# Plain strips in place of some 2x2 sum pairs, and another order of chunks, in a two-layer decoder kernel

## Chip, cores and metric

The kernel runs on one core of a Trainium2 chip. The metric is the device time of one execution in microseconds (us). The engines are TensorE (PE in the profile, with its weight loads as PEld), VectorE (DVE), ScalarE (ACT), GpSimd (POOL) and SyncE (SP), which issues the loads.

## What is computed

Two decoder layers over 256 tokens of width 2048, all in f32:

```python
for i in range(DEPTH):                      # DEPTH = 2
    h = rms_norm(x, pre_mix_gain[i])
    m = hybrid_mixer(h, ...)                # h @ w_in, attention and a gated recurrence, @ w_out
    x = x + rms_norm(m, post_mix_gain[i])
    h = rms_norm(x, pre_ffn_gain[i])
    f = (silu(h @ w_ffn_gate[i]) * (h @ w_ffn_up[i])) @ w_ffn_down[i]     # width 5632
    x = x + rms_norm(f, post_ffn_gain[i])
    gate = sigmoid(rms_norm(x, ple_gain[i]) @ w_ple_gate[i])
    x = x + (p[i] @ w_ple_proj[i]) * gate
```

## The kernel before

The 256 tokens are two tiles of 128 (`t` = 0, 1). The activations of a product stand transposed in SBUF (`xT`, four tiles `ck` of four 128-row blocks each, split into a high and a low part); they are the stationary operand, and weights stream past them. A weight **chunk** is 256 rows by 512 columns, 512 KB, loaded by SyncE into `wr` (6 buffers). ScalarE rounds it to the high part `wh` (L281), VectorE subtracts that to get the low part `wl` (L291); both have 7 buffers. One product of a chunk with one token tile is two blocks times three matmuls (high by high, low by high, high by low): 6 matmuls of 128x512.

`strip` (L306 to L309) makes 512 output columns: for each chunk, 6 matmuls for `t` = 0 and 6 for `t` = 1, in two PSUM banks `acc0` and `acc1`. With `skew=n` the second tile lags n chunks behind the first. At the end of each tile it calls `done(t, ps)`.

`paired` (L361) makes two such strips at once and saves one product in eight on the first two chunks of the two strips, by sums of blocks, in the manner of Strassen and Winograd. Its part `fast` (L398) takes four chunks, `r11`, `r12`, `r21`, `r22`, and forms four differences of them (`sub`, L396, VectorE, written over `wr`). It splits seven operands instead of four (L281 and L291), and takes sums of activation blocks that `mixed` (L332) made once per stage (L343, L349, L179, L180). It makes seven products of 6 matmuls into four banks `accc`, `acce`, `acca`, and two of the pool `ms` (rows `ms<-wh,sum` and `ms<-wh,ck`). Three results are copied out (L389), two are added (L426, L427). The part `plain` (L430) does the other chunks of each strip like `strip`. At the end `summed` (L357) adds what was copied out to the bank before `done` goes on. So one pair of nch chunks a strip has 4 nch - 1 products: 186 matmuls at nch = 8, 138 at nch = 6, 90 at nch = 4, where two strips would have 192, 144 and 96.

Each layer runs these stages in order: eleven strips of `w_in` with attention and recurrence between them; `w_out` as two pairs; the gated blocks `gated(n)`, n = 0 to 10, each a pair of a gate strip and an up strip; after blocks 2, 4, 7 and 10 the down product of that group of 2, 3, 3 and 3 blocks, as two pairs (columns s = 0, 1 and s = 2, 3; nch is 4 in the first group and 6 in the others); and the stage called PLE here, `w_ple_gate`, as two pairs, each with two short strips `projected` of 12 matmuls for p.

At two places of a layer the new activations come only from what has just ended: `post_norm` (L465) needs the squares of the whole row (L175 on ScalarE, sums and a power on GpSimd), then scales and adds on VectorE (L470), and `next_in` transposes the result on TensorE (L201, 32 blocks, tiles x_84 to x_87 for t = 0 and x_88 to x_91 for t = 1) and splits it (L208 on ScalarE, L210 on VectorE). This is so between `w_out` and the first gated block, and between the last down product and PLE. Such work is put off by `later(n, ...)`, n ticks of the chunk loop. In the first pair after such a border (`first=False`) `plain` of the first strip ran ahead of `fast`, from chunk 2 on and with skew 5, and the sums came 6 ticks later.

A gated block's result goes through DRAM to be transposed (`shuffled`), and is split at L179 and L180 into the `ck` tiles of the down product.

The program is written in this order, and a scheduler then places each engine's instructions; within that order it moves matmuls past one another where it expects a wait.

Of the kernel before, what the change touches and what calls it, by code (L numbers as in the profile page):

```python
# [17 lines left out]
NT = 2  # L18
# [29 lines left out]
def decoder(ctx: ExitStack, tc: tile.TileContext, x, p, positions, w_in, attn_sinks,  # L48
# [312 lines left out]
    def paired(lhs, sums, wa, wb, cols, done_a, done_b, nch=8, row0=0, first=True,  # L361
               skews=(0, 0), after=None):
# [35 lines left out]
        def fast(bank_e, bank_a):  # L398
# [11 lines left out]
            e = bank_e or psum("acce")  # L410
# [10 lines left out]
            a = bank_a or psum("acca")  # L421
# [8 lines left out]
        def plain(w, col, banks, skew, end):  # L430
            n = nch - 2
            ws = {}
            for i in range(n + skew):
                if i < n:
                    ws[i] = load_w(w, base + 2 + i, col)
                    acc(banks[0], block(2 + i, 0), ws[i])
                    if i == n - 1:
                        end(0)
                if i >= skew:
                    acc(banks[1], block(2 + i - skew, 1), ws[i - skew])  # L440
                tick()
            end(1)

        if first:
            e, a, c, x1, x2 = fast(None, None)
            if after:
                after()
            plain(wa, cols[0], (e, a), skews[0], lambda t: done_a(t, (e, a)[t], x1[t]))
        else:
            e, a = psum("acce"), psum("acca")  # L450
            plain(wa, cols[0], (e, a), skews[0], lambda t: None)
            e, a, c, x1, x2 = fast(e, a)
            for t in range(NT):
                done_a(t, (e, a)[t], x1[t])
            if after:
                after()
        d = psum("accd")
        plain(wb, cols[1], (c, d), skews[1], lambda t: done_b(t, (c, d)[t], x2[t]))
# [204 lines left out]
    for l in range(DEPTH):  # L663
# [427 lines left out]
        def gated(n, last, first):  # L1091
# [21 lines left out]
            paired(xT, lambda: sx[0], w_ffn_gate[l], w_ffn_up[l], (col, col), summed(done_gate),  # L1113
                   summed(done_up), first=n > 0, skews=(0 if n else SKEW, 0))

        for gi, glen in enumerate(FF_GROUPS):
# [11 lines left out]
            for s in range(4):  # L1128
# [37 lines left out]
        px = []  # L1166
        later(6, lambda: px.append(mixed(xT[0], ("kv", "A"))))

# [4 lines left out]
        def gate_of(s, pj):  # L1173
# [23 lines left out]
            return summed(done)  # L1197
# [38 lines left out]
```

## Time and profile before

| | |
|---|---|
| median of 2 runs | 2414.31 us (2413.87 to 2414.75) |
| the profiled execution | 2413.03 us, of which the span of instructions is 2411.3 us |
| PE busy | 2373.9 us, 98% of the span |
| PEld busy | 1955.5 us, 81% |
| DVE busy | 2044.5 us, 85% |
| ACT busy | 1382.8 us, 57% |
| DMA | 497.64 MB, mean 206 GB/s |

Busy is the share of the span in which an engine has an instruction under way. Matmuls overlap in the pipeline, so a busy PE need not be going at its full rate; the distance between the starts of two matmuls shows that.

### The profile page before, as it was taken

The page shows a single profiled execution, that of the slowest core. Times are in us where ns is not written, and L with a number is a line of the kernel's source. Part 1 is how long each engine was busy: PE and PEld are TensorE (multiplying, and loading weights), DVE is VectorE, ACT ScalarE, POOL GpSimd, SP SyncE. Part 2 cuts the span into 40 slices and gives each one's busy share as a digit, 9 for nine tenths or more (in the row PEclk, how much of TensorE's full clock was granted, in tenths as well). Part 3 has the DMA queues.
Part 4 walks back from the last instruction along what each step waited for, and adds up shares of the span by engine and source line. Part 5 has one row for each costly group of instructions (what it writes and reads, how often), then busy time and mean ns, then how long its engine had stood idle before and what let it go on. Part 6 is the DMA issues. An engine that isn't in the chain of part 4 may idle for free.

```text
span 2411.3 us, 31504 instructions
## 1 busy us (share of the span) xinstructions
PE 2373.9 (98%) x10975; PEld 1955.5 (81%) x10975; DVE 2044.5 (85%) x2689; ACT 1382.8 (57%) x1954; POOL 103.8 (4%) x213
## 2 busy tenths in 40 slices
PE   9999999999999999999999999999999999999999
PEld 7888887888888888877788888878888888888777
DVE  7687987899997898899877879788998988888996
ACT  6555466656555555557556554565555555555664
POOL 3100001000000000001010000010000000000010
PEclk9999999999999999999999999999999999999999
DMA  8666464776667666665776564746667576666744
GB/s 295 212 193 201 137 223 137 237 225 221 206 207 248 195 216 221 226 215 166 238 223 213 174 218 134 234 134 220 220 218 219 198 248 195 209 230 213 232 153 150
DMA packets 299360, 497.64 MB, mean 206 GB/s; under 512 B 23456, under 2 KB 69440, under 8 KB 299200
## 3 DMA queue, kind: packets, MB, share of 16 engines
q1 hardware_dynamic: 298896, 495.54, 63.5%
q8 instruction: 86, 1.41, 0.2%
q14 instruction: 74, 0.61, 0.1%
q10 hardware_dynamic: 240, 0.07, 0.0%
q0 software_dynamic: 64, 0.02, 0.0%
HBM read 470.38 MB, written 25.17 MB: 206 GB/s over the span
## 4 chain that ended last, share of the span: by engine, by line
PE 84%; DVE 9%; DMA 3%; ACT 2%; issue 2%; SPq 1%; POOL 0%; DVEq 0%; ACTq 0%; POOLq 0%
PE acc L306 7%; PE acc L307 7%; PE acc L309 6%; PE accc L383 5%; PE accc L384 5%; PE accc L380 5%; PE acca L383 5%; PE acca L384 5%; PE acca L380 5%; PE acce L384 4%; PE acce L380 4%; PE acce L383 4%; PE accd L383 4%; PE accd L384 4%; PE accd L380 4%; DVE wl L291 3%
## 5 line engine op out<-in xcount | busy, mean ns | idle before, releaser
L281 ACT CAST wh<-wr 128x1024 fp32r<-128x1024 f32 x978 | 1009.9, 1052 | 784.5 <-DVE wr L396 262.5
L291 DVE TENSOR_TENSOR wl<-wr,wh 128x1024 fp32r<-128x1024 f32 x978 | 1167.1, 1220 | 222.8 <-ACT wh L281 208.3
L306 PE MATMUL acc<-wh,ck 128*128 128x512 f32 x704 | 278.2, 395 | 0.8 <-ACT ck L179 0.8
L307 PE MATMUL acc<-wh,ck 128*128 128x512 f32 x704 | 275.5, 392 | 0.0
L309 PE MATMUL acc<-wl,ck 128*128 128x512 f32 x704 | 275.0, 391 | 0.0
L396 DVE TENSOR_TENSOR wr<-wr 128x1024 f32<-128x1024 f32 x184 | 225.0, 1223 | 6.8 <-DMA wr<-in_w_ffn_down_dram 1.7
L380 PE MATMUL acca<-wh,ck 128*128 128x512 f32 x564 | 222.6, 395 | 6.3 <-ACT wh L281 4.8
L383 PE MATMUL acca<-wh,ck 128*128 128x512 f32 x564 | 221.5, 393 | 3.5 <-DVE ck L180 1.8
L383 PE MATMUL acce<-wh,ck 128*128 128x512 f32 x564 | 220.6, 391 | 3.6 <-DVE ck L210 3.4
L380 PE MATMUL acce<-wh,ck 128*128 128x512 f32 x564 | 220.8, 392 | 0.4 <-ACT wh L281 0.4
L384 PE MATMUL acca<-wl,ck 128*128 128x512 f32 x564 | 221.0, 392 | 0.0
L384 PE MATMUL acce<-wl,ck 128*128 128x512 f32 x564 | 219.9, 390 | 0.3
L380 PE MATMUL accd<-wh,ck 128*128 128x512 f32 x472 | 184.0, 390 | 0.0
L380 PE MATMUL accc<-wh,ck 128*128 128x512 f32 x472 | 183.9, 390 | 0.0
L383 PE MATMUL accd<-wh,ck 128*128 128x512 f32 x472 | 183.8, 389 | 0.0
L383 PE MATMUL accc<-wh,ck 128*128 128x512 f32 x472 | 183.8, 389 | 0.0
L384 PE MATMUL accd<-wl,ck 128*128 128x512 f32 x472 | 183.7, 389 | 0.0
L384 PE MATMUL accc<-wl,ck 128*128 128x512 f32 x472 | 183.6, 389 | 0.0
L306 PEld LDWEIGHTS acc<-wh,ck 128*128 128x128 f32 x704 | 132.1, 188 | 27.6 <-ACT ck L179 1.0
L309 PEld LDWEIGHTS acc<-wl,ck 128*128 128x128 f32 x704 | 132.2, 188 | 27.4
L307 PEld LDWEIGHTS acc<-wh,ck 128*128 128x128 f32 x704 | 132.3, 188 | 27.0 <-DVE ck L180 0.4
L380 PEld LDWEIGHTS acca<-wh,ck 128*128 128x128 f32 x564 | 106.4, 189 | 33.8 <-ACT wh L281 9.7
(272 smaller groups left out, 3510.9 us busy)
## 6 DMA issues: line engine op xcount, KB each, us to landing
wr<-in_w_in_dram SPq DMA_DIRECT2D x176, 512.0 KB, 4.9
wr<-in_w_ffn_gate_dram SPq DMA_DIRECT2D x176, 512.0 KB, 4.5
wr<-in_w_ffn_up_dram SPq DMA_DIRECT2D x176, 512.0 KB, 5.9
wr<-in_w_ffn_down_dram SPq DMA_DIRECT2D x176, 512.0 KB, 5.2
wr<-in_w_out_dram SPq DMA_DIRECT2D x64, 512.0 KB, 4.7
wr<-in_w_ple_gate_dram SPq DMA_DIRECT2D x64, 512.0 KB, 5.5
turn<-nat SPq DMA_DIRECT2D x86, 256.0 KB, 2.6
nat<-turn SPq DMA_DIRECT2D x344, 64.0 KB, 3.3
```

The lines of the kernel that those rows point to most:

```text
L281: marks["hi"] = S.copy(hi, raw)
L291: marks["lo"] = V.tensor_tensor(lo, raw, hi.bitcast(F32), op=ALU.subtract)
L306: T.matmul(ps[t], xh, hi[:, k], start=first, stop=False)
L307: T.matmul(ps[t], xl, hi[:, k], start=False, stop=False)
L309: marks[t, c] = marks["pe"] = T.matmul(ps[t], xh, lo[:, k], start=False, stop=last)
L380: T.matmul(ps, xh, hi[:, k], start=id(ps) not in opened, stop=False, skip_group_check=True)
L383: T.matmul(ps, xl, hi[:, k], start=False, stop=False, skip_group_check=True)
L384: marks["pe"] = T.matmul(ps, xh, lo[:, k], start=False, stop=k == 1, skip_group_check=True)
L396: V.tensor_tensor(dst, p, q, op=ALU.subtract)
```

## The change

Five edits, all in the order and the kind of the products:

1. Gated block 0 of each layer is a gate strip (skew 5), then the sums of the stage, then an up strip, in place of a pair with `plain` first.
2. In the last group's down product the columns s = 2 and s = 3 are strips of their own (skew 0 and 4), in place of a pair. `done` adds the bank to `macc` first, and what was copied out afterwards, where there is any.
3. PLE columns s = 0 and s = 1 are strips of their own (skew 5 and 0), in place of a pair. The sums are made after the first.
4. In the remaining PLE pair both `projected` strips of p come after `fast`; before, one came ahead of it.
5. In the down pair s = 0, 1 of each group `plain` goes over all chunks but the last two of both strips, and then over the last two of both (`mixed_order`). The last two chunks meet the gated block that was made last. At nch = 4 this changes nothing.

`first=False` is gone with its two users.

```diff
-    def paired(lhs, sums, wa, wb, cols, done_a, done_b, nch=8, row0=0, first=True,
-               skews=(0, 0), after=None):
+    def paired(lhs, sums, wa, wb, cols, done_a, done_b, nch=8, row0=0, skews=(0, 0),
+               after=None, mixed_order=False):
...
-        else:
-            e, a = psum("acce"), psum("acca")
-            plain(wa, cols[0], (e, a), skews[0], lambda t: None)
-            e, a, c, x1, x2 = fast(e, a)
...
+        if mixed_order:
+            d = psum("accd")
+            plain(wa, cols[0], (e, a), 0, None, c1=nch - 2)
+            plain(wb, cols[1], (c, d), 0, None, c1=nch - 2)
+            plain(wa, cols[0], (e, a), 0, end_a, c0=nch - 2)
+            plain(wb, cols[1], (c, d), 0, end_b, c0=nch - 2)
+            return
...
             if n == 0:
-                later(6, lambda: sx.append(mixed(xT[0], ("kv", "at"))))
+                strip(xT, w_ffn_gate[l], col, done_gate, skew=SKEW)
+                sx.append(mixed(xT[0], ("kv", "at")))
+                strip(xT, w_ffn_up[l], col, done_up)
+                return
...
-                    V.tensor_tensor(x, ps, x, op=ALU.add)
-                    V.tensor_tensor(m, x, m, op=ALU.add)
+                    V.tensor_tensor(m, ps, m, op=ALU.add)
+                    if x is not None:
+                        V.tensor_tensor(m, x, m, op=ALU.add)
...
-                if s % 2:
+                if last and s >= 2:
+                    strip(hid, w_ffn_down[l], s * W, lambda t, ps, done=done: done(t, ps, None),
+                          nch=2 * glen, row0=ff0 * W, skew=4 if s == 3 else 0)
+                elif s % 2:
                     paired(hid, lambda: hx[0], w_ffn_down[l], w_ffn_down[l], (s * W - W, s * W),
                            dones[s - 1], done, nch=2 * glen, row0=ff0 * W,
-                           skews=(0, 4 if last and s == 3 else 0))
+                           mixed_order=s == 1)
...
-        for s in (0, 2):
-            pa, pb = [], []
+        for s in (0, 1):
+            pa = []
             projected(s, pa)
-            paired(xT, lambda: px[0], w_ple_gate[l], w_ple_gate[l], (s * W, s * W + W),
-                   gate_of(s, pa), gate_of(s + 1, pb), first=s > 0,
-                   skews=(0, SKEW) if s else (SKEW, 0), after=lambda: projected(s + 1, pb))
+            strip(xT, w_ple_gate[l], s * W, gate_of(s, pa), skew=SKEW if s == 0 else 0)
+            if s == 0:
+                px = mixed(xT[0], ("kv", "A"))
+        pa, pb = [], []
+
+        def project():
+            projected(2, pa)
+            projected(3, pb)
+        paired(xT, lambda: px, w_ple_gate[l], w_ple_gate[l], (2 * W, 3 * W),
+               summed(gate_of(2, pa)), summed(gate_of(3, pb)), skews=(0, SKEW), after=project)
```

What stands where now, at three places.

TensorE at the start of the first gated block of layer 0, before: the bank `acce` is the first strip's tile t = 0, and its first matmuls read `ck` made from x_85, that is chunk 2.

```order
L201 MATMUL ms<-ident,x_86 128x128 [waits DVE_49]
L201 MATMUL ms<-ident,x_86 128x128 x3
L380 MATMUL acce<-wh,ck 128x512 [waits Activation_49]
L383 MATMUL acce<-wh,ck 128x512 [waits DVE_49]
L384 MATMUL acce<-wl,ck 128x512
```

And now, further on in the same strip, where the second token tile (x_88 on, bank acc_3839) begins; chunk 0 of the strip reads `ck` made from x_84.

```order
L309 MATMUL acc_3838<-wl,ck 128x512 [waits DVE_49]
L201 MATMUL ms<-ident,x_88 128x128 [waits DVE_49]
L201 MATMUL ms<-ident,x_88 128x128 x3
L201 MATMUL ms<-ident,x_89 128x128 [waits DVE_49]
L201 MATMUL ms<-ident,x_89 128x128 x3
L306 MATMUL acc_3838<-wh,ck 128x512 [waits Activation_49]
L307 MATMUL acc_3838<-wh,ck 128x512
L309 MATMUL acc_3838<-wl,ck 128x512
L306 MATMUL acc_3839<-wh,ck 128x512 [waits Activation_49]
L306 MATMUL acc_3838<-wh,ck 128x512
L307 MATMUL acc_3838<-wh,ck 128x512
L309 MATMUL acc_3838<-wl,ck 128x512 [waits DVE_49]
```

The strip starts with the block that was ready first. Its x_88 transposes stand behind 33 matmuls of the strip; before, they stood behind 28.

VectorE in the same stage before, where the sums (L349 and the `sum` rows of L180) and the differences (L396) are made:

```order
L349 TENSOR_TENSOR nat<-nat 128x256 [waits DVE_49]
L396 TENSOR_TENSOR wr<-wr 128x1024 [waits DMAHW0_49]
L349 TENSOR_TENSOR nat<-nat 128x256 [waits DVE_49]
L180 TENSOR_TENSOR sum<-nat,sum 128x512 [waits Activation_49]
L396 TENSOR_TENSOR wr<-wr 128x1024 [waits DMAHW2_49,DVE_49]
L180 TENSOR_TENSOR sum<-nat,sum 128x512 [waits Activation_49]
L291 TENSOR_TENSOR wl<-wr,wh 128x1024 [waits PE_49]
```

and now, in the up strip of the same block:

```order
L291 TENSOR_TENSOR wl<-wr,wh 128x1024 [waits DMAHW7_49,PE_49,Activation_49]
L343 TENSOR_TENSOR nat<-ck 128x512 [waits DVE_49] x2
L291 TENSOR_TENSOR wl<-wr,wh 128x1024 [waits DMAHW0_49,PE_49,Activation_49]
L349 TENSOR_TENSOR nat<-nat 128x256 [waits DVE_49]
L349 TENSOR_TENSOR nat<-nat 128x256
L349 TENSOR_TENSOR nat<-nat 128x256 [waits DVE_49]
L291 TENSOR_TENSOR wl<-wr,wh 128x1024 [waits DMAHW1_49,PE_49,Activation_49]
```

The sums and differences no longer stand between a pair's own products and the weights that these wait for; they lie among the low parts of a strip, and six low parts stand ahead of them.

TensorE in the down pair s = 0, 1 of the second group in layer 1, at the first use of the last gated block for t = 1, before:

```order
L380 MATMUL acca<-wh,ck 128x512 [waits Activation_49]
L383 MATMUL accc<-wh,ck 128x512
L384 MATMUL accc<-wl,ck 128x512
L384 MATMUL accd<-wl,ck 128x512
L383 MATMUL acca<-wh,ck 128x512 [waits DVE_49]
L384 MATMUL acca<-wl,ck 128x512
```

and now:

```order
L384 MATMUL acce<-wl,ck 128x512
L380 MATMUL acca<-wh,ck 128x512 [waits Activation_49]
L383 MATMUL acca<-wh,ck 128x512 [waits DVE_49]
L384 MATMUL acca<-wl,ck 128x512
```

The matmul that waits for VectorE there is the 89th of the stage before and the 98th now: the scheduler had already put products of the second strip ahead of it.

More of the change, by code (lines that the diff above doesn't have):

```diff
@@ L409, in fast @@
             tick()
[L410 removed]
+            e = psum("acce")
             acc(e, block(1, 0), parts(r21))
@@ L428, in fast, with plain @@
             return e, a, c, (p1, u3), (u2, p5)
-        def plain(w, col, banks, skew, end):
-            n = nch - 2
+        def plain(w, col, banks, skew, end, c0=2, c1=nch):
+            n = c1 - c0
             ws = {}
@@ L434, in plain, with end_a, end_b @@
                 if i < n:
-                    ws[i] = load_w(w, base + 2 + i, col)
-                    acc(banks[0], block(2 + i, 0), ws[i])
-                    if i == n - 1:
+                    ws[i] = load_w(w, base + c0 + i, col)
+                    acc(banks[0], block(c0 + i, 0), ws[i])
+                    if i == n - 1 and end:
                         end(0)
                 if i >= skew:
-                    acc(banks[1], block(2 + i - skew, 1), ws[i - skew])
+                    acc(banks[1], block(c0 + i - skew, 1), ws[i - skew])
                 tick()
[L442 to L448, printed above, removed]
-        else:
-            e, a = psum("acce"), psum("acca")
-            plain(wa, cols[0], (e, a), skews[0], lambda t: None)
-            e, a, c, x1, x2 = fast(e, a)
[L453 to L456, printed above, removed]
+            if end:
+                end(1)
+        e, a, c, x1, x2 = fast()
+        if after:
+            after()
+        def end_a(t):
+            done_a(t, (e, a)[t], x1[t])
+        def end_b(t):
+            done_b(t, (c, d)[t], x2[t])
+        if mixed_order:
[5 more added lines that the diff above has]
+            return
+        plain(wa, cols[0], (e, a), skews[0], end_a)
         d = psum("accd")
-        plain(wb, cols[1], (c, d), skews[1], lambda t: done_b(t, (c, d)[t], x2[t]))
+        plain(wb, cols[1], (c, d), skews[1], end_b)
     def load_gain(g, col):
```

10 lines of the change are left out of this document (4 added, 6 removed).

## Prediction

> **What bounds the kernel now.** First the page's busy times:
>
> ```profile
> PE 2373.9 (98%) x10975; PEld 1955.5 (81%) x10975; DVE 2044.5 (85%) x2689; ACT 1382.8 (57%) x1954; POOL 103.8 (4%) x213
> ```
>
> TensorE is busy nearly throughout. Whether it also goes at its full rate shows in its timeline (start, duration) at the start of gated block 9, far from any border:
>
> ```profile
> 946.20 0.39 PE L380 MATMUL ms<-wh,ck 128*128 128x512 f32 x1
> 946.42 0.39 PE L383 MATMUL ms<-wh,ck 128*128 128x512 f32 x1
> ```
>
> Starts lie 0.22 to 0.23 us apart, though each matmul is drawn as 0.39. So a stage of n matmuls cannot take less than 0.2267 n, and what a stage takes beyond that is the place to look. The busy times by stretch, one stretch a stage (start:end, length, then busy time and instructions of each engine, granted clock, DMA share, GB/s):
>
> ```profile
> core 0: us, PE busy (x) PEld busy (x) DVE busy (x) ACT busy (x) POOL busy (x), PEclk, DMA share, GB/s
> 946.20:988.36 42.16, 42.16 (x188) 34.92 (x186) 34.45 (x37) 23.67 (x26) 0.00 (x0) 1.00 0.68 224
> 872.74:904.04 31.30, 31.30 (x140) 25.91 (x138) 29.75 (x31) 16.64 (x18) 0.00 (x0) 1.00 0.64 212
> 389.83:440.24 50.41, 46.14 (x210) 36.57 (x207) 48.83 (x77) 35.69 (x69) 6.14 (x13) 1.00 0.47 158
> 440.24:483.82 43.58, 43.01 (x187) 34.69 (x186) 37.00 (x38) 24.25 (x27) 0.00 (x0) 1.00 0.71 229
> 1030.52:1063.21 32.69, 32.24 (x144) 26.06 (x142) 28.04 (x34) 18.20 (x23) 0.00 (x0) 1.00 0.70 223
> 1063.21:1097.90 34.69, 32.99 (x149) 26.46 (x148) 32.93 (x39) 22.54 (x35) 4.84 (x7) 1.00 0.78 257
> 1097.90:1156.29 58.39, 54.61 (x237) 42.56 (x236) 54.63 (x86) 42.32 (x85) 6.94 (x13) 0.97 0.46 151
> 1156.29:1210.54 54.25, 50.09 (x211) 40.33 (x210) 45.15 (x61) 33.08 (x53) 0.86 (x4) 0.97 0.73 234
> 1210.54:1233.26 22.72, 22.72 (x105) 18.75 (x104) 18.38 (x40) 14.65 (x29) 3.76 (x8) 1.00 0.63 196
> 1588.84:1640.85 52.01, 47.72 (x210) 37.71 (x208) 49.35 (x77) 35.71 (x69) 6.84 (x13) 0.97 0.49 161
> 1640.85:1684.03 43.18, 42.76 (x187) 34.69 (x186) 36.50 (x38) 24.26 (x27) 0.00 (x0) 1.00 0.68 222
> 1853.13:1885.98 32.85, 31.97 (x139) 25.67 (x138) 27.35 (x32) 17.04 (x19) 0.00 (x0) 1.00 0.63 205
> 2043.78:2076.12 32.34, 31.72 (x140) 25.75 (x139) 27.35 (x32) 17.13 (x19) 0.00 (x0) 1.00 0.66 208
> 2233.89:2266.01 32.12, 32.00 (x144) 26.04 (x142) 27.94 (x34) 18.27 (x23) 0.00 (x0) 1.00 0.69 226
> 2266.01:2300.93 34.92, 33.00 (x150) 26.46 (x147) 32.75 (x39) 22.63 (x35) 4.54 (x7) 1.00 0.75 249
> 2300.93:2357.67 56.74, 52.98 (x237) 41.41 (x235) 53.81 (x85) 40.01 (x77) 6.96 (x13) 1.00 0.45 149
> ```
>
> The first two are references: gated block 9 (186 matmuls, 42.16, so 0.2267 each) and a down pair (138, 31.30). Both take the matmul time exactly, the second with VectorE busy for 29.75 of its 31.30. In a steady stage, then, VectorE's load costs nothing. The others run longer. Layer 0: block 0 (the row from 389.83) 8.25 over, block 1 1.42, last down pairs 1.41 and 3.41, PLE pairs 10.79 and 6.65 over 210 matmuls with their projections. Layer 1: block 0 9.85, block 1 1.02, down pairs s = 0, 1 of groups 1, 2 and 3 1.57, 1.06 and 0.84, the last pair 3.64, first PLE pair 9.14. Together 59.05. The row 1210.54 is the strip after PLE, 96 matmuls and 8 transposes: 22.72 is 0.96 over, so 0.12 a transpose. The rows above hold 56 transposes a layer (20, 4, 8, 24): 13.4 in all, which stay. That leaves **45.6 us of stalls**. What TensorE waits for (total, times, longest):
>
> ```profile
> PE ms L380 <- ACT wh L281: 7.6, 10, 1.4
> PE acca L380 <- ACT wh L281: 4.8, 11, 0.6
> PE acce L383 <- DVE ck L210: 3.4, 2, 1.7
> PE ms L380 <- DVE nat L1180: 2.3, 1, 2.3
> PE acca L383 <- DVE ck L180: 1.8, 3, 0.9
> PE ms L201 <- DVE x L470: 1.6, 2, 0.9
> ...
> PE acca L380 <- ACT ck L208: 1.6, 2, 0.8
> PE acca L383 <- DVE ck L210: 1.3, 2, 0.7
> ```
>
> The largest are for rounded weights, in the products of `fast`; then those for new activations at the borders (L208, L210, L470), for a bank (L1180), and for the last gated block (L180). Each listed wait costs 0.16 more than it says, since the last matmul before it is drawn that much past its step. The rest of the 45.6 is clock:
>
> ```profile
> 1130.00:1133.30 3.30, 1.64 (x7) 1.00 0.78 239
> 1133.30:1136.70 3.40, 3.40 (x8) 0.51 0.78 248
> 1170.90:1174.30 3.40, 3.40 (x10) 0.50 0.94 282
> 1621.40:1624.90 3.50, 3.50 (x10) 0.51 0.85 262
> ```
>
> Three times, after 3 to 5 us in which TensorE stood half the time (1.64 of 3.30 in the first row), the granted clock was 0.50 for 3.4 us: 1.7 us lost each, **5.1** in all, inside those 45.6.
>
> **What it costs.** Three pairs a layer become strips: 6 matmuls more each, 36 in all, 36 x 0.2267 = **+8.2 us**. They sit on the engine that is the bound, and nothing hides them. The loads are the same bytes; the projections are the same.
>
> **What it takes off VectorE and ScalarE.**
>
> ```profile
> L281 ACT CAST wh<-wr 128x1024 fp32r<-128x1024 f32 x978 | 1009.9, 1052 | 784.5 <-DVE wr L396 262.5 <-PE acc L307 120.9 <-PE acca L383 105.3
> L291 DVE TENSOR_TENSOR wl<-wr,wh 128x1024 fp32r<-128x1024 f32 x978 | 1167.1, 1220 | 222.8 <-ACT wh L281 208.3 <-PE ms L384 5.7 <-PE ms L383 2.6
> L396 DVE TENSOR_TENSOR wr<-wr 128x1024 f32<-128x1024 f32 x184 | 225.0, 1223 | 6.8 <-DMA wr<-in_w_ffn_down_dram 1.7 <-DMA wr<-in_w_ple_gate_dram 0.5
> ```
>
> A pair's three extra operands cost 3 x 1.052 on ScalarE and 3 x 1.220 on VectorE, its four differences 4 x 1.223: 8.55 us of VectorE in a stretch of seven products, 42 x 0.2267 = 9.5 us, which with the four ordinary splits asks 13.4 us of it. That is why `fast` starves unless six or seven operands were made before. L281's idle time says the same: 262.5 us of it ended with a difference. Directly behind a border nothing can be made ahead, since VectorE is full of the border's own work; the strips give 2.72 us of products for each 1.22.
>
> **Stage by stage, what stays.**
>
> Gated block 0. The first stall (2 us in each layer, `acce` for L210) goes: the strip begins with the chunk whose activations were ready, and comes to the later ones with more matmuls between. TensorE then reaches x_88 sooner, but VectorE does not:
>
> ```profile
> 395.41 1.12 DVE L210 SCALAR_TENSOR_TENSOR ck<-ms,gT,ck 128x128 fp32r<-128x128 f32 x4
> 396.45 0.68 DVE L1074 TENSOR_TENSOR mg<-nat,gB 128x512 f32<-128x512 f32 x1
> 397.05 2.74 DVE L470 SCALAR_TENSOR_TENSOR x<-mg,po,x 128x512 f32<-128x512 f32 x4
> ```
>
> Before, this L210 group of x_87 stood behind the addition that opens the chain of t = 1 (L357); now it stands ahead of it. The chain starts 1.1 later and its square and power follow, so x_88, the first of the four L470 (0.69 each), comes at about 398.5 in place of 397.8. From 389.83, 33 matmuls and 4 transposes bring TensorE there at 397.8: 0.7 lost. The two transposed tiles cost 0.2 more. The low part of the next chunk stands behind all four L470, until 401.7 against 400.9: 0.8. The first L210 for t = 1 follows: 0.3. With 0.16 for each of three, **2.5 a layer stays** of 8.25 - 2.4 and 9.85 - 2.4. The sums lie in the up strip, with six low parts ahead. Block 1's `fast` finds its operands made: 0.3 stays of 1.42 and 1.02.
>
> Down pairs s = 0, 1. The matmul that waits for the last gated block is 9 matmuls later, 2.0 us against waits of at most 0.9: 0.1 stays of each. A new wait could stand at the end of the last: the strip s = 2 opens in the bank of `accc`, read by L1147 on VectorE behind two `done` and two low parts. From the end of `acce` two low parts and five additions, 2 x 1.22 + 5 x 0.69 = 5.9 us, go first there, and TensorE needs 30 matmuls and 4 transposes, 7.3: cover enough by a little. If not, one 0.69 us addition a layer is exposed.
>
> Last down strips and PLE column 0. Between the last matmul of t = 0 and the transposes of x_84 lie 24 matmuls now and 22 before, and the chain is one addition (0.69) shorter; today TensorE waits there for L470, 0.9 at most: 0.4 stays of 3.41 - 1.0 and 3.64 - 1.0. In PLE column 0 TensorE reaches x_88 some 7 us after the last down matmul, the chain about 5 after it. The L210 of t = 1 stand behind four older tiles' and come as TensorE does: between 0 and 2.3, what the same place loses now; I take 1.5, since the gated block's border keeps more. The PLE pair's `fast` starts behind a strip of 21.8 us with VectorE free for half of it, and its two `ms` banks were left by a strip's end, not a pair's: 0.5 stays of 6.65. In layer 1 that pair has no stall today and should have none.
>
> Stays: 2.5 + 0.3 + 0.1 + 0.4 + 1.5 + 0.5 = 5.3 in layer 0 and 2.5 + 0.3 + 0.3 + 0.4 + 1.5 = 5.0 in layer 1, 10.3 in all. So 45.6 - 10.3 = **35.3 go and 8.2 come: -27.1**. The profiled execution took 2413.03, 1.7 of it outside the span, which stays; 2413.03 - 27.1 = **2386**. It lies 1.3 below the median of the runs shown, within their noise.
>
> **The clock again.** [...] I count none, since block 0 of layer 0 has its 8.25 over at a clock of 1.00.
>
> **Rivals.** *All stalls go* (0.10): 2413.0 - 45.6 + 8.2 = 2376. For: the chains at PLE come out level above.
>
> *The borders are latency, not load* (0.22): the four waits for x and ck stay and grow by the 2 us that TensorE arrives sooner. 9.2 today (7.9 listed in L210, L208 and L470, with 0.16 each), 8 more, three clock drops 5.1, the rest 2.3: 24.6 stay, 2413.0 - 21.0 + 8.2 = 2400. For: VectorE goes from 395.41 to 399.8 without a gap in the rows above. Against: its queue there held weights that are not on the chain.
>
> *The new chunk order does little* (0.03): the scheduler had already moved other products ahead, so 4 us of the down pairs stay: 2390.
>
> *VectorE is the bound* (0.02). [...] As a mechanism of this kernel: 6 x 8.55 us of differences and splits and 6 x 6 additions of 0.69, 76 us, would come off the time, and the 36 matmuls would hide: 2337. Against: the down pair at 95% VectorE loses nothing.
>
> *Slower* (0.03): the ring of seven weight buffers. A strip with skew 5 holds six chunks for t = 1 while it asks for the eighth, which must wait for the first to be given back; `plain` had six chunks and fitted. If TensorE waits there for a round through ScalarE, four L210 pairs and VectorE, 1.05 + 2.15 + 1.22 = 4.4, and a clock drop of 1.7 follows, four skewed strips cost 24.4, and with 8.2 32.6. It decides if less than 32.6 of the stalls go; with 28 gone, 2418. Against: at that point TensorE has other matmuls of t = 1 before it.
>
> **How the numbers follow.** 2386 has 0.60. The range goes from all stalls gone, 2376, to 2401, the second rival and one us more; what lies outside are the last two rivals and about half of the second and of the first, 0.2 in all. About 2% (48 us) is what a measurement here tells from no change; since stalls are 45.6, faster by more needs the VectorE rival: 0.02; slower by more 0.01.
>
> **What would show it.** Right: block 0's two strips together 46 to 49 us in place of 50.4 and 52.0; PLE's first two columns together 53 to 55 (they do 216 matmuls, 49.0); the last PLE pair in layer 0 within a us of 47.6; waits on L281 under 3 us in all; no or one stretch at clock 0.5. Wrong: waits of TensorE for L210 and L470 above 10 us in all, or `acc` waiting for L291 at a strip's eighth chunk.

## The result, and the profile after

| | before | after |
|---|---|---|
| median of 2 runs | 2414.31 us | 2387.69 us (2386.98 to 2388.40) |
| ratio of the times | | 0.989, interval 0.985 to 0.993 |
| profiled execution, its span | 2413.03, 2411.3 us | 2388.40, 2386.7 us |

The change makes the kernel 1.1% faster, by 26.6 us between the medians and 24.6 us between the two profiled spans. The prediction was 2386. The page's busy times after:

```profile
PE 2370.5 (99%) x11011; PEld 1963.0 (82%) x11011; DVE 1977.1 (83%) x2611; ACT 1356.6 (57%) x1918; POOL 102.7 (4%) x213
```

TensorE has 36 matmuls more and is busy 3.4 us less: that row alone would not have shown a gain of 24.6, since a matmul that is drawn 0.39 long, at a step of 0.2267, covers the first 0.16 of a stall. VectorE has 78 instructions and 67 us less. The busy times by stretch show where it went (start:end, length, then busy time and instructions of each engine, granted clock, DMA share, GB/s):

```profile
392.43:418.67 26.24, 24.92 (x120) 19.93 (x119) 22.04 (x46) 22.51 (x54) 6.29 (x13) 1.00 0.57 177
418.67:440.43 21.76, 21.76 (x98) 18.02 (x97) 18.88 (x23) 9.92 (x11) 0.00 (x0) 1.00 0.53 176
440.43:483.02 42.59, 42.45 (x188) 34.84 (x186) 33.41 (x35) 23.65 (x26) 0.00 (x0) 1.00 0.69 223
683.42:716.12 32.70, 31.88 (x139) 25.76 (x138) 32.03 (x34) 18.51 (x20) 0.00 (x0) 1.00 0.62 203
873.90:905.55 31.65, 31.59 (x140) 25.82 (x139) 31.06 (x32) 17.80 (x21) 0.00 (x0) 1.00 0.62 211
1032.02:1063.90 31.88, 31.88 (x143) 26.13 (x142) 26.38 (x31) 20.03 (x25) 0.00 (x0) 1.00 0.87 281
1063.90:1097.88 33.98, 33.81 (x155) 27.73 (x154) 23.22 (x30) 17.54 (x29) 3.83 (x7) 1.00 0.62 198
1097.88:1150.73 52.85, 52.13 (x244) 42.90 (x243) 49.44 (x84) 38.02 (x82) 7.90 (x13) 1.00 0.59 184
1150.72:1198.66 47.94, 47.94 (x211) 39.19 (x210) 38.85 (x52) 31.70 (x50) 1.01 (x4) 1.00 0.80 258
1576.99:1603.26 26.27, 24.95 (x119) 19.94 (x118) 22.08 (x46) 22.50 (x54) 6.30 (x13) 1.00 0.56 177
1625.02:1667.18 42.16, 42.16 (x187) 34.91 (x186) 33.41 (x35) 23.85 (x26) 0.00 (x0) 1.00 0.69 225
1866.98:1898.62 31.64, 31.58 (x140) 25.83 (x138) 30.61 (x31) 17.66 (x20) 0.00 (x0) 1.00 0.62 205
2056.38:2088.21 31.83, 31.64 (x139) 25.83 (x138) 31.25 (x32) 17.91 (x21) 0.00 (x0) 1.00 0.63 209
2280.28:2333.12 52.84, 52.12 (x244) 42.88 (x243) 47.00 (x75) 35.37 (x70) 7.89 (x13) 1.00 0.53 171
```

In layer 0 these are, from the top: the gate strip and the up strip of block 0 (48.00 together, a pair of 50.41 before), block 1 (42.59, from 43.58), the down pairs s = 2, 3 of groups 2 and 3 (at 683.42 and 873.90), the last group's pair s = 0, 1 (31.88, from 32.69), its two strips s = 2 and 3 (33.98, from 34.69), PLE columns 0 and 1 (52.85, from a pair of 58.39), and the PLE pair (47.94, from 54.25). The last five rows are layer 1: gate strip, block 1, the down pairs s = 2, 3 of groups 2 and 3, PLE columns 0 and 1. The lengths show the gain, and **four rows show a loss**: the down pairs s = 2, 3 of groups 2 and 3, which took 31.28 to 31.30 before, now take 31.64 to 32.70. (The four groups of a layer are counted from 1 here; the prediction's sum counts them from 0.) What TensorE waits for (total, times, longest; L475 is the former L470):

```profile
PE ms L201 <- DVE x L475: 2.1, 4, 0.9
PE ms L380 <- ACT wh L281: 1.6, 3, 0.8
...
PE ms L201 <- DVE ck L210: 1.4, 2, 0.7
PE acca L380 <- ACT wh L281: 1.0, 4, 0.3
PE acc L309 <- DVE wl L291: 0.8, 2, 0.4
```

The waits for rounded weights (L281) fell from 12.4 in the prediction's two rows, 13.2 with two smaller ones, to 2.6; those for new activations (L210 and L475) are 3.5. None is for the bank of `accc`, and none for L1189, the former L1180.

With the prediction's prices (0.2267 a matmul, 0.12 a transpose) what stays of the stalls is 2.1 in each block 0, 0.4 in block 1 of layer 0 (0 in layer 1), 0.1 in the pair at 1032.02, 0.4 in each layer's last down strips (33.95 us in layer 1), 1.0 in each PLE column pair and 0.3 in the PLE pair: 7.8 of 45.6, so 37.8 went. The matmuls brought 8.2, the four down pairs 2.7, and the first strip of the kernel 2.3. That is -24.6, the difference of the spans. The 2.3 have nothing to do with the change; the same five microseconds at the start, before and after:

```profile
10.00:15.00 5.00, 5.00 (x28) 4.20 (x27) 4.51 (x7) 4.14 (x8) 0.10 (x4) 1.00 1.04 369
```

```profile
10.00:15.00 5.00, 5.00 (x19) 3.99 (x19) 2.82 (x4) 1.96 (x5) 0.10 (x4) 1.00 1.01 332
```

TensorE does 19 matmuls and transposes there in place of 28. Until about 14 us its matmuls start 0.43 us apart (five steps from 10.26 to 12.39), as they do in a stretch of half clock (six steps from 1133.82 to 1136.38 in the profile before), though the clock column says 1.00 there. The same kernel in another profile, and other kernels below, had 25.4 to 27.0 us for that strip, in no order that follows the change.

### The profile page after: what moved, and what is told of

Same layout as the page of the kernel before. It is cut to its first block, busy times and chain, and to the rows that moved or that the text cites. A ratio compares the mean times of both kernels' runs of the same rounds, so it can differ in the third digit from the quotient of the medians.

```text
span 2386.7 us, 31506 instructions
## 1 busy us (share of the span) xinstructions
PE 2370.5 (99%) x11011; PEld 1963.0 (82%) x11011; DVE 1977.1 (83%) x2611; ACT 1356.6 (57%) x1918; POOL 102.7 (4%) x213
## 4 chain that ended last, share of the span: by engine, by line
PE 86%; DVE 8%; DMA 2%; issue 1%; ACT 1%; POOL 1%; SPq 0%; ACTq 0%; DVEq 0%; POOLq 0%
PE acc L307 9%; PE acc L306 9%; PE acc L309 9%; PE accc L384 5%; PE accc L383 5%; PE accc L380 5%; PE acca L380 4%; PE acca L383 4%; PE acca L384 4%; PE acce L380 4%; PE acce L384 4%; PE acce L383 4%; PE accd L380 3%; PE accd L384 3%; PE accd L383 3%; DVE wl L291 3%
## 5 line engine op out<-in xcount | busy, mean ns | idle before, releaser
L281 ACT CAST wh<-wr 128x1024 fp32r<-128x1024 f32 x960 | 995.2, 1053 | 821.8 <-DVE wr L396 239.6
L291 DVE TENSOR_TENSOR wl<-wr,wh 128x1024 fp32r<-128x1024 f32 x960 | 1145.3, 1218 | 265.9 <-ACT wh L281 255.1
L306 PE MATMUL acc<-wh,ck 128*128 128x512 f32 x1056 | 418.1, 396 | 0.3 <-ACT ck L179 0.3
L307 PE MATMUL acc<-wh,ck 128*128 128x512 f32 x1056 | 413.5, 392 | 0.0
L309 PE MATMUL acc<-wl,ck 128*128 128x512 f32 x1056 | 412.4, 392 | 0.8 <-DVE wl L291 0.8
L309 PEld LDWEIGHTS acc<-wl,ck 128*128 128x128 f32 x1056 | 198.8, 188 | 43.2 <-DVE wl L291 1.7
L307 PEld LDWEIGHTS acc<-wh,ck 128*128 128x128 f32 x1056 | 199.0, 188 | 40.2 <-DVE ck L180 0.5
L306 PEld LDWEIGHTS acc<-wh,ck 128*128 128x128 f32 x1056 | 198.8, 188 | 40.4 <-ACT ck L179 0.8
L396 DVE TENSOR_TENSOR wr<-wr 128x1024 f32<-128x1024 f32 x160 | 195.8, 1224 | 6.4 <-DMA wr<-in_w_ffn_down_dram 1.7
L380 PE MATMUL acca<-wh,ck 128*128 128x512 f32 x488 | 190.5, 390 | 1.1 <-ACT wh L281 1.0
L383 PE MATMUL acce<-wh,ck 128*128 128x512 f32 x488 | 190.0, 389 | 0.0
L383 PE MATMUL acca<-wh,ck 128*128 128x512 f32 x488 | 190.0, 389 | 0.0
L384 PE MATMUL acca<-wl,ck 128*128 128x512 f32 x488 | 189.9, 389 | 0.0
L380 PE MATMUL acce<-wh,ck 128*128 128x512 f32 x488 | 189.8, 389 | 0.0
L384 PE MATMUL acce<-wl,ck 128*128 128x512 f32 x488 | 189.8, 389 | 0.0
L380 PE MATMUL accd<-wh,ck 128*128 128x512 f32 x408 | 159.1, 390 | 0.0
L383 PE MATMUL accd<-wh,ck 128*128 128x512 f32 x408 | 158.7, 389 | 0.0
L380 PE MATMUL accc<-wh,ck 128*128 128x512 f32 x408 | 158.7, 389 | 0.0
L383 PE MATMUL accc<-wh,ck 128*128 128x512 f32 x408 | 158.7, 389 | 0.0
```

Of the source, the lines that this page charges most:

```text
L281: marks["hi"] = S.copy(hi, raw)
L291: marks["lo"] = V.tensor_tensor(lo, raw, hi.bitcast(F32), op=ALU.subtract)
L306: T.matmul(ps[t], xh, hi[:, k], start=first, stop=False)
L307: T.matmul(ps[t], xl, hi[:, k], start=False, stop=False)
L309: marks[t, c] = marks["pe"] = T.matmul(ps[t], xh, lo[:, k], start=False, stop=last)
L380: T.matmul(ps, xh, hi[:, k], start=id(ps) not in opened, stop=False, skip_group_check=True)
```

## The experiments

Each kernel is the changed one with one edit, twice with two. They ran in four groups on four chips, each with the kernel before beside it, whose median there was 2413.30 to 2414.73. All times are medians, ratios are to the kernel before. Five rounds leave about 3 us of uncertainty in a ratio, so each verdict rests on the stages in the profile first.

**The base.** The changed kernel once more.

> The changed kernel again, as the base for the other three on the same chip. Both theories: 2387.7 us, ratio to the kernel before 0.989.

2387.48 us, ratio 0.989 (0.987 to 0.990). Its four down pairs s = 2, 3 take 31.65, 31.64, 31.64 and 31.64, its PLE pair in layer 0 takes 49.20. The 32.70 and 47.94 above were thus single draws: these stages differ by about a microsecond between two executions of one program. "The control" below is this run.

**Edit 1 undone**

```diff
-                strip(xT, w_ffn_gate[l], col, done_gate, skew=SKEW)
-                sx.append(mixed(xT[0], ("kv", "at")))
-                strip(xT, w_ffn_up[l], col, done_up)
-                return
+                later(6, lambda: sx.append(mixed(xT[0], ("kv", "at"))))
...
-                   summed(done_up))
+                   summed(done_up), first=n > 0, skews=(0 if n else SKEW, 0))
```

> Edit 1 undone: the first gated block is a pair again, plain first. My theory (a strip gives VectorE 2.72 us of products for each split, and the pair behind a border asks too much of it): +8.4 us against the control, from the blocks 0 and 1 together, 93.99 and 95.19 us before against 90.59 and 90.19 after. Rival (the border costs latency, the same in both forms): -2.7 us, the 12 matmuls of 0.2267 us that the pair saves in two layers.

2393.81 us, +6.3 against the control. Block 0 of layer 0, and block 0 and block 1 of layer 1:

```profile
389.81:440.19 50.38, 46.10 (x209) 36.56 (x207) 48.80 (x77) 35.67 (x69) 6.83 (x13) 1.00 0.49 158
1577.48:1627.91 50.43, 46.15 (x210) 36.57 (x208) 48.86 (x77) 35.68 (x69) 6.19 (x13) 1.00 0.49 158
1627.91:1671.44 43.53, 42.74 (x187) 34.68 (x186) 36.85 (x38) 24.36 (x27) 0.00 (x0) 1.00 0.69 229
```

The pair takes 2.4 us more than the two strips though it has 6 matmuls less, and block 1 behind it 1.3 and 1.4 more: 7.5 in the four stages. VectorE is busy 48.8 of 50.4. My 8.4 held the half clock that block 0 of layer 1 had before (52.01 at a mean clock of 0.97) and has not here. The latency rival, -2.7, falls. Two of the four waits of TensorE in the first of these stages:

```profile
392.00 0.50 PE L383 MATMUL acce<-wh,ck 128*128 128x512 f32 x1 [1.72 <-DVE ck L210]
420.21 0.50 PE L380 MATMUL ms<-wh,sum 128*128 128x512 f32 x1 [1.39 <-ACT wh L281]
```

The first is for the activations of chunk 2, with which this form of the pair begins. The second is for a rounded weight, with 0.53 for a low part before it and 0.53 for another weight behind it. So 1.7 of the pair's waits belong to the order of its chunks, and 2.4 to the operands that `fast` asks for. The run undoes both at once, and no run separates them.

**Edit 2 undone**

```diff
-                if last and s >= 2:
-                    strip(hid, w_ffn_down[l], s * W, lambda t, ps, done=done: done(t, ps, None),
-                          nch=2 * glen, row0=ff0 * W, skew=4 if s == 3 else 0)
-                elif s % 2:
+                if s % 2:
...
-                           mixed_order=s == 1)
+                           mixed_order=s == 1, skews=(0, 4 if last and s == 3 else 0))
```

> Edit 2 undone: the last down columns s = 2, 3 are a pair again. My theory: +1.7 us against the control by the stage alone (34.69 and 34.92 us before, 33.97 and 33.95 after), up to +2.5 with a later start of PLE. Rival (latency): -2.7 us, the 12 matmuls saved.

2394.24 us, **+6.8**, three times what I expected. The last down pairs, layer 0 and layer 1:

```profile
1060.58:1098.08 37.50, 35.04 (x149) 27.26 (x148) 34.76 (x42) 23.98 (x36) 4.53 (x7) 0.95 0.72 245
2247.18:2285.18 38.00, 35.09 (x149) 27.46 (x148) 34.79 (x42) 23.84 (x36) 4.54 (x7) 0.96 0.70 235
```

Not 34.7 and 34.9 as before the change, but 37.5 and 38.0. VectorE at the start of that pair in layer 0:

```profile
1060.76 0.68 DVE L1147 TENSOR_TENSOR macc<-accc,macc 128x512 f32<-128x512 f32 x1
1061.36 0.68 DVE L1147 TENSOR_TENSOR macc<-accd,macc 128x512 f32<-128x512 f32 x1
1061.96 1.28 DVE L1149 TENSOR_TENSOR macc<-nat,macc 128x512 f32<-128x512 f32 x2
...
1067.61 2.48 DVE L396 TENSOR_TENSOR wr<-wr 128x1024 f32<-128x1024 f32 x2
```

The `done`s of the pair s = 0, 1 lie at the start of the next pair, and the last two of that pair's four differences come only at 1067.6 to 1070.1, and TensorE, which had waited 0.5 us for a low part just before, waits 1.1 us for the first of them. A half clock of 3.4 us follows, in each layer. That led to the next test.

**Edits 2 and 5 undone together**: the edit above, with `mixed_order=False`.

> Edits 2 and 5 undone together. With edit 2 alone undone the last down columns s = 2, 3 took 37.51 and 38.00 us, with both edits in 33.98 and 33.96, and before the change 34.69 and 34.92. My theory (the two edits depend on each other: with the last two chunks at the end, the ends of all four tiles of s = 0, 1 fall into the start of the next pair): the pair s = 2, 3 takes 34.7 to 34.9 us again without either edit, and the whole lies 1.7 to 2.7 us above the run with edit 5 alone undone, 2391 to 2392. Rival (the pair costs what it costs, whatever stands ahead of it): 37.5 to 38.0 us in that pair, 2396.

2391.76 us, and the pair again without a half clock:

```profile
1062.89:1097.60 34.71, 33.00 (x150) 26.46 (x148) 32.93 (x39) 22.63 (x35) 4.87 (x7) 1.00 0.75 257
2249.16:2283.83 34.67, 32.96 (x149) 26.47 (x148) 32.91 (x39) 22.53 (x35) 4.83 (x7) 1.00 0.74 250
```

34.71 and 34.67: as my theory has it. Edit 2 is worth 2.5 us between the medians where edit 5 is absent (2391.76 against the 2389.31 below; 0.7 in each layer by the stage alone) and 6.8 where it is present (3.5 and 4.0 by the stage, the half clock's 1.7 in each included). **The edits depend on each other**: the late chunks make a pair behind them dear, and a strip does not mind.

**Edits 3 and 4 undone**

```diff
-        for s in (0, 1):
-            pa = []
+        for s in (0, 2):
+            pa, pb = [], []
             projected(s, pa)
-            strip(xT, w_ple_gate[l], s * W, gate_of(s, pa), skew=SKEW if s == 0 else 0)
...
+            paired(xT, lambda: px[0], w_ple_gate[l], w_ple_gate[l], (s * W, s * W + W),
+                   summed(gate_of(s, pa)), summed(gate_of(s + 1, pb)), first=s > 0,
+                   skews=(0, SKEW) if s else (SKEW, 0), after=lambda: projected(s + 1, pb))
```

> Edits 3 and 4 undone: PLE is two pairs again, the first with plain first, one projection of p ahead of fast. My theory: +15.8 us against the control (112.64 and 110.38 us before, 100.78 and 106.41 after), of which up to 3.4 us is a half clock in layer 0 that need not come again. Rival (latency): -2.7 us.

2397.06 us, +9.6. The two PLE pairs of layer 0:

```profile
1093.89:1148.89 55.00, 51.94 (x237) 41.55 (x236) 53.73 (x85) 40.16 (x79) 6.70 (x13) 1.00 0.50 164
1148.89:1203.30 54.41, 50.06 (x212) 40.32 (x210) 45.33 (x61) 34.48 (x56) 0.86 (x4) 0.97 0.75 238
```

The second pair is as before the change (54.25), half clock included. The first is not: 55.00 and, in layer 1, 54.98, against 58.39 and 56.74. One half clock (1.7 us) explains part of it in layer 0. The other 1.7 in each layer probably came from what stands ahead of it, edits 2 and 5; no run tests that alone. Latency, -2.7, falls here too.

More than half of the +9.6 is in the second pair of layer 0, 54.41 against 49.20 in the control. TensorE's two longest waits in it:

```profile
1158.30 0.50 PE L380 MATMUL ms<-wh,sum 128*128 128x512 f32 x1 [2.44 <-DVE nat L1200]
1162.60 0.50 PE L380 MATMUL ms<-wh,sum 128*128 128x512 f32 x1 [1.30 <-ACT nat L389]
```

L1200 is the former L1180: VectorE multiplies the gate by the projection of p, which lies in the `ms` bank that TensorE wants next. L389 is ScalarE's copy out of such a bank. VectorE works without a gap from 1143 to 1166, and the copy stands behind roundings that wait for its differences. So here VectorE's load reaches TensorE by way of two banks that come free late; a half clock follows. Whether it is edit 3 or edit 4 that frees them stays open, since the two were undone together.

**Edit 5 undone**

```diff
-                           mixed_order=s == 1)
+                           mixed_order=False)
```

> Edit 5 undone: in the down pairs s = 0, 1 plain goes through the first strip and then the second. My theory: about +1.3 us against the control (2400 or so less 11): 4.0 us of waits for the last gated block come back in the pairs s = 0, 1, and 2.7 us go from the pairs s = 2, 3 behind them, whose differences no longer stand behind four bunched done. Rival (the scheduler makes the chunk order alone idle): 0 in both.

2389.31 us, ratio 0.990 (0.989 to 0.991): +1.8, near the 1.3 expected but within the uncertainty. The profile is clearer. The down pairs of group 2 in layer 0 (s = 0, 1, then s = 2, 3), and the last group's s = 0, 1:

```profile
649.02:681.44 32.42, 31.88 (x139) 25.76 (x138) 27.62 (x32) 16.93 (x19) 0.00 (x0) 1.00 0.64 209
681.44:712.72 31.28, 31.28 (x139) 25.92 (x138) 29.41 (x30) 16.63 (x18) 0.00 (x0) 1.00 0.63 208
1028.94:1062.75 33.81, 32.33 (x143) 25.99 (x142) 28.44 (x34) 19.52 (x24) 0.00 (x0) 1.00 0.73 226
```

The waits for the last gated block are back (32.42 and 33.81, from 31.28 and 31.64 in the control), and the loss in s = 2, 3 is gone (31.28), with VectorE busy there for 29.41 in place of 31.2. Over the three groups in both layers edit 5 gains 5.4 in the pairs s = 0, 1 and loses 1.4 in the others, 4.0 net by the stages. So the scheduler had not already made the chunk order idle, and the new loss is from edit 5.

**The copied-out part added early**

```diff
-                    if x is not None:
-                        V.tensor_tensor(m, x, m, op=ALU.add)
...
         e, a, c, x1, x2 = fast()
+        if early:
+            early(x1, x2)          # adds x1[t], x2[t] to macc
```

> In groups 2 to 4 the copied-out part is added to macc right behind fast, so that each done of a down pair is one addition of 0.69 us and not two. My theory (eight bunched additions delay the differences of the next pair): the pairs s = 2, 3 of groups 2 and 3 come to 31.3 us each, from 32.70, 31.65, 31.64 and 31.83: up to -2.5 us against the control. Rival (the stall is from the ring of weights or the loads): 0.

2386.00 us, ratio 0.989 (0.987 to 0.990): no difference. The four pairs take 33.19, 31.67, 31.43 and 32.65, no better than the control. Counted from the start of the first of them, VectorE ends its last differences 7.2 us in, 6.3 in the control, since one of the pair's own early additions now stands ahead of them and VectorE waits twice for a rounded weight; and TensorE comes to the product over the changed `r22` at 5.5 us in place of 6.6, since the order of the products moved too. So the run is a miss as a test of what the additions cost. It shows something else: in its four pairs the last differences end 7.2, 5.6, 5.4 and 6.6 us in, and the loss over 31.28 is 1.9, 0.4, 0.2 and 1.4 us, in the same order.

**GpSimd adds the copied-out part** in groups 2 and 3:

```diff
-                        V.tensor_tensor(m, x, m, op=ALU.add)
+                        (V if last else G).tensor_tensor(m, x, m, op=ALU.add)
```

> In groups 2 and 3 GpSimd, not VectorE, adds the copied-out part to macc (eight additions of 0.69 us a group less on VectorE; GpSimd has 4 per cent of its time in use). My theory (VectorE's backlog at the border of the two down pairs makes the differences of the next pair late): the pairs s = 2, 3 of these groups take 31.3 us each, with no loss, in place of 31.64 to 32.70, so -1.3 to -2.5 us against the control. Rival (not the backlog but the loads or the ring of weights): 31.6 or more each, 0.

2399.51 us, **+12.0**. The four pairs take 35.07, 36.26, 35.38 and 33.76. The second and the third hold a half clock of 1.7 each. GpSimd and VectorE at the border ahead of the first pair, and TensorE in it:

```profile
675.54 3.52 POOL L1149 TENSOR_TENSOR macc<-nat,macc 128x512 f32<-128x512 f32 x2 [267.54 <-DVE macc L1147]
```

```profile
675.31 0.68 DVE L1147 TENSOR_TENSOR macc<-acca,macc 128x512 f32<-128x512 f32 x1
675.91 2.01 DVE L291 TENSOR_TENSOR wl<-wr,wh 128x1024 fp32r<-128x1024 f32 x1
677.85 2.31 DVE L396 TENSOR_TENSOR wr<-wr 128x1024 f32<-128x1024 f32 x1
```

```profile
688.42 0.50 PE L380 MATMUL ms<-wh,nat 128*128 128x512 f32 x1 [2.93 <-ACT wh L281]
```

One addition takes 1.3 to 2.2 us on GpSimd. While the first two run (675.54 to 679.06), VectorE's L291 and L396 take 2.01 and 2.31 us in place of 1.22 (in the profile after, all 960 L291 take 1.18 to 1.24 and all 160 L396 1.21 to 1.23); both read two operands from SBUF. The L1147 ahead of them, with one operand from PSUM and GpSimd at work beside it for its last 0.45, takes its 0.68. So VectorE loses 1.9 us there to be rid of two additions of 0.69, its last differences end at 688.5, and TensorE waits 2.93 us. My expectation left this out. Whether it is the place of the operands that decides, no run tests. The theory that VectorE's backlog holds TensorE up agrees in direction, not in the way that I meant. The same pair (group 2, layer 0, s = 2, 3) in five executions, by the end of VectorE's last differences after the pair's start:

| | last differences end | the pair takes |
|---|---|---|
| edit 5 undone | 4.9 us | 31.28 us |
| control | 6.3 | 31.65 |
| early addition | 7.2 | 33.19 |
| the changed kernel, profile after | 7.3 | 32.70 |
| GpSimd additions | 8.6 | 35.07 |

The two go together, though not strictly across kernels whose products stand in another order (7.2 and 7.3).

**Far from a border: two strips for a pair.** Gated blocks 5, 6, 8 and 9 as strips:

```diff
+            if n in (5, 6, 8, 9):
+                strip(xT, w_ffn_gate[l], col, done_gate)
+                strip(xT, w_ffn_up[l], col, done_up)
+                return
```

> Gated blocks 5, 6, 8 and 9, far from any border, are two strips each in place of a pair: 6 matmuls more and 8.55 us of VectorE less, 8 times. My theory (only TensorE's count matters there): +10.9 us against the control, 48 x 0.2267, nothing hidden. Rival (VectorE is the bound): 8 x (8.55 + 4 x 0.69) = about 90 us faster.

2397.94 us, +10.5 against the control. Block 5 of layer 0:

```profile
712.32:755.84 43.52, 43.52 (x193) 36.05 (x192) 22.00 (x21) 18.15 (x19) 0.00 (x0) 1.00 0.69 205
```

192 matmuls in 43.52, 1.36 more than the pair, which is 6 x 0.2267: the matmuls count in full, and the 11.6 us that VectorE is spared (22.0 for 33.6) bring nothing.

**Far from a border: more work for VectorE**, the opposite:

```diff
         marks["lo"] = V.tensor_tensor(lo, raw, hi.bitcast(F32), op=ALU.subtract)
+        if again:                  # five times in blocks 5, 6, 8 and 9
+            again.pop()
+            marks["lo"] = V.tensor_tensor(lo, raw, hi.bitcast(F32), op=ALU.subtract)
```

> In gated blocks 5, 6, 8 and 9 five low parts each are computed twice by VectorE (the same instruction again, 1.22 us): 8 x 5 x 1.22 = 48.8 us more on VectorE, whose busy time there goes from 34.5 to 40.6 of 42.2 us. My theory (in a steady stage VectorE's load costs nothing as long as it fits): within 1 us of the control. Rival (VectorE is the bound): +48.8 us.

2386.89 us, 0.6 under the control: no difference. Block 8 of layer 0:

```profile
900.70:942.86 42.16, 42.16 (x188) 34.92 (x186) 39.99 (x40) 23.34 (x25) 0.00 (x0) 1.00 0.66 213
```

VectorE busy for 95% of a stage that still takes 42.16. With the run before it, VectorE as the bound is out in a steady stage; near a border the same engine, as full, does cost time, because there its work has a date.

**Skew 6** in the gate strip of block 0 and in PLE column 0:

```diff
-                strip(xT, w_ffn_gate[l], col, done_gate, skew=SKEW)
+                strip(xT, w_ffn_gate[l], col, done_gate, skew=SKEW + 1)
```

> The strips behind a border (gate strip of block 0, PLE column 0) with skew 6 in place of 5: TensorE comes to x_88 12 matmuls, 2.7 us of work, later. My theory (what stays at the four borders, 2 x 2.19 and 2 x 1.50 us, is waiting for the second token tile): up to -3.5 us against the control. Rival (a ring of seven weight buffers, of which the lagging tile then holds seven): 0, or slower by a round through ScalarE and VectorE, some 4 us a border.

2387.42 us, the same as the control; the gate strip takes 26.51 in place of 26.23. TensorE in it, skew 5 (the control) and skew 6, and VectorE at skew 6:

```profile
400.39 1.32 PE L201 MATMUL ms<-ident,x 128*128 128x128 f32 x8 [0.89 <-DVE x L475]
```

```profile
400.24 1.32 PE L201 MATMUL ms<-ident,x 128*128 128x128 f32 x8 [0.90 <-DVE x L475]
```

```profile
396.02 0.67 DVE L357 TENSOR_TENSOR nat<-accd,nat 128x512 f32<-128x512 f32 x1
...
399.43 2.74 DVE L475 SCALAR_TENSOR_TENSOR x<-mg,po,x 128x512 f32<-128x512 f32 x4 [1.01 <-POOL po L170]
```

The wait for x_88 is the same 0.9, for the transposes stand behind 33 matmuls of the strip in both: the scheduler places them there whatever the skew, so my theory did not get the 2.7 us that it counted on. Nor does the ring cost its 4.4 a border. What sets the wait is the chain: it opens at 396.0 with L357, some five microseconds after the last matmul of `accd`, and then VectorE stands idle for 1.0 us until GpSimd's power (L170).

**Both, the early addition and skew 6**

> The earlier addition and skew 6 together. If both causes are as I have them, the sum of the two: up to -6 us against the control, near 2382. If either is wrong, what the other gives alone.

2390.12 us, 2.6 over the control. The four pairs take 33.11, 32.18, 32.51 and 32.48, 3.7 more than the control's in all. Neither part had done what it was meant to, and the sum of the two is no gain. No version here beats the changed kernel.

## Why the prediction was right, and where it was not

**The total** is right to 2 us, and part of that is luck. Between the two profiles, less stays than I had counted (2.5 us); edit 5 costs 2.7 that I had left out; and 2.3 came by accident at the start of the kernel: -27.1 - 2.5 + 2.7 + 2.3 = -24.6. The signs that I had named came out, but for the first two PLE columns: block 0's two strips took 48.00 and 48.03, the last PLE pair 47.94 (49.20 in the control is outside), L281 is waited for 2.6, and no stage holds a half clock.

**What bounds the kernel** held: the time is TensorE's matmuls at 0.2267 and what it waits for. The two runs far from a border show both halves of it, +1.36 us for six matmuls and nothing for 6 us of VectorE. The +8.2 is therefore the real price of the change.

**Why the strips help** held as far as the runs separate it: undoing edit 1 adds 2.4 us to each block 0, and undoing edits 3 and 4 adds 2.2 to each first PLE pair, though 6 matmuls go each time. The latency rival (2400) needed a loss of nothing there and is refuted. Its grain of truth is the 1.0 us in which VectorE waits for the power. But relief of VectorE is not the whole of it: with edit 1 undone 1.7 us of the waits come from the order of the chunks. And the largest single gain, in the last PLE pair of layer 0, comes by way of banks. The prediction had named both.

**What stays** is 7.8 us against my 10.3. Block 0: 2.1 against 2.5, at the places named: in each layer a wait of 0.89 for x_88 and one of 0.42 for the low part behind the four L475. Block 1: 0.4 and 0, against 0.3 twice. The last down strips: 0.4 in each layer, as predicted. PLE column 0: 1.0 against 1.5, a bounded guess; so the first two PLE columns took 52.85 where I had asked for 53 to 55. The PLE pair: 0.3 against 0.5, but 1.6 in the control (49.20), so this term is no better known than to a microsecond. The wait that I feared for the bank of `accc` is not there.

**The step that failed is edit 5.** I counted its gain, the waits for the last gated block (0.1 stays; measured 0.1 or less), and looked for the late thing only at the bank of `accc` in the last group. I did not ask what the ends of four tiles, all behind one another, do to the stage behind them: the four pairs s = 2, 3 of groups 2 and 3 lose 2.7 us in the profile after, 1.4 in the control, nothing without edit 5. In the last group the same would have cost 2.8 to 3.3 us in each layer, had edit 2 not put strips there (37.50 and 38.00 against 34.71 and 34.67; 1.7 of each is a half clock). I took the five edits as independent terms of a sum, and these two are not. That the loss goes with the lateness of the next pair's differences shows in the four pairs of the early addition; how much of that lateness the bunched additions make stays open, since neither of the two attempts to move them changed that alone.

**The clock.** I counted no half clock, and none is in the stages after; the 5.1 us of before went with the stalls. The 2.3 us at the start of the kernel, where TensorE went at half its rate (0.43 us a step) for longer, were not in the sum.

**The other rivals.** *VectorE is the bound* (2337) fell with the two runs far from a border: at 95% it cost nothing (42.16). TensorE's weight-load busy time reads 83% in stages that go matmul behind matmul (34.92 of 42.16, 36.05 of 43.52), so 82% over the span is no room of 18%: here it has to be read against 83% and not against 100%. *The chunk order does little* fell: 5.4 us of waits come back without edit 5, though the net is 4.0. *The ring of weights*: no wait of `acc` for L291 above 0.4, and skew 6, which holds one buffer more, costs 0.3 a gate strip and not 4.4.

## What to carry to other kernels

Beside a border, where an engine's results are due at a date, price a saved product by what it asks of the engine that prepares its operands: here saving one product of 32 (1.36 us), with the order of chunks that came with it, made a stage 2.1 to 2.4 us longer. Far from a border the saved product counted in full here (43.52 us for two strips, 42.16 for the pair), and a VectorE at 95% cost nothing (42.16 again). When work is moved to the end of a stage to let a wait pass, list everything that the end of the stage releases at once and see what the next stage wants from that engine first; and test edits in pairs, since one may only pay because another is there.

## What the runs showed of the hardware

**The half clocks lay on a grid of 3.413 us.** In the profile before, the three stretches of half clock lasted 3.41 us each and began at 1133.35, 1170.89 and 1621.45: 37.55 and 450.56 us apart, 11.0 and 132.0 times 3.413 (450.56 / 132). In the run with edit 2 undone the two began 1187.84 apart, 348.0 times, and with the GpSimd additions 996.7, 292.0 times. The stretch of 3.41 us before a half clock and the half clock itself, edit 2 undone, layer 0:

```profile
1066.52:1069.93 3.41, 1.76 (x7) 0.80 (x5) 3.34 (x3) 1.04 (x1) 0.00 (x0) 1.00 0.74 220
1069.93:1073.34 3.41, 3.34 (x7) 2.23 (x8) 3.41 (x4) 2.94 (x3) 0.00 (x0) 0.50 0.69 213
```

TensorE was idle for 48% of the stretch ahead; in layer 1 it was the same (1.76 busy of 3.41). In the profile before, the stretch ahead of 1133.35 was idle for 49%, in two waits of 1.14 and 0.53 us. Leaving out the first and the last microseconds of a run, all eight half clocks of four runs (before, edit 2 undone, edits 3 and 4 undone, GpSimd additions) follow a stretch of the grid that was idle for 47 to 84%. No stretch there with less brought one. But four with 50 to 53% brought none either. One of them, in the profile before:

```profile
1164.06:1167.47 3.41, 1.67 (x6) 1.05 (x6) 3.41 (x5) 1.84 (x2) 0.00 (x0) 1.00 0.60 172
```

So within a run a stretch that was about half idle brought a half clock in some places and none in others. Near the start it took less: with skew 6, and with skew 6 and the early addition, a half clock at 8.3 and 9.4 us followed stretches idle for 46 and 38%. What exactly decides stays open. Whether a stall paid the 1.7 us on top thus differed between executions: block 0 of layer 1 took 52.01 with a half clock in the profile before, and the same pair took 50.43 without one with edit 1 undone.

**VectorE was slower beside GpSimd's additions**, where both read two operands from SBUF: two operations of VectorE that took 1.18 to 1.24 us in the profile after took 2.01 and 2.31 at one border of the run with the GpSimd additions. What makes them slower was not tested.
